# Operands of three products stored as high and low parts by one phase and loaded by the next, and one set of inner weights formed in place

## The chip, the core and the metric

The kernel runs on one core of a Trainium2 chip. The metric is device time in microseconds (us) of one launch; the median of the runs shown is what counts. The core has a matrix engine (PE; its weight loads are listed as PEld), a vector engine (DVE), a scalar engine (ACT), GpSimd (POOL) and SyncE (SP). SP, ACT and POOL can issue transfers between DRAM and the on-chip memory; each engine works through its own instructions in order and waits on semaphores.

## The reference, cut to what matters

```python
def rms_norm(x, w):
    xf = x.astype(jnp.float32)
    y = xf * lax.rsqrt(jnp.mean(xf * xf, axis=-1, keepdims=True) + RMS_EPS)
    return (y * w.astype(jnp.float32)).astype(x.dtype)

def pool_mixer(h, in_w, group_w, group_b, scale, out_w):
    b, s, _ = h.shape
    u, gate = jnp.split(h @ in_w, 2, axis=-1)
    ug = u.reshape(b, s, POOL_GROUPS, POOL_GROUP_DIM)
    pooled = jnp.stack([trailing_mean(ug[:, :, g], w) for g, w in enumerate(POOL_WINDOWS)],
                       axis=2) - ug
    mixed = jnp.einsum('bsgc,gcd->bsgd', pooled, group_w) + group_b
    y = mixed.reshape(b, s, POOL_WIDTH) * scale * jax.nn.silu(gate)
    return y @ out_w
```

There is one layer: h = x + pool_mixer(rms_norm(x, norm_w), ...), and the output is rms_norm(h, final_norm_w). The input has 4096 rows of 1024 float32 values; `in_w` is 1024 x 2048, `out_w` 1024 x 1024, and the trailing windows are 2, 4, 8 and 16 rows long. The mixer's group map is folded into the first half of `in_w`.

## The kernel before, in words

**Precision.** A float32 matmul is made of three: each operand is split into a high part (an ACT copy to float32r) and a low part (a DVE subtraction), and `mm3` adds high x high, high x low and low x high. `split` (L154) does this for one tile of 128 x 1024, with its ACT copy on L152 and its DVE subtraction on L146 (helpers: all ACT copies stand on L152, all DVE subtractions on L146, all additions on L143, all products of two tiles on L149).

**Seven products.** Each matrix product of 2 x 2 blocks is done with seven products instead of eight (the Strassen-Winograd scheme), called P1 to P7. On the data side the sums are S3 (P7), S2 (P6), S1 (P5) and S4 (P3); P1, P2 and P4 take blocks as they are. The code keeps the blocks in `xs[b]` under "11", "12", "21" (which becomes S3), "22" and "2" (S2); "11" becomes S1 and "12" becomes S4, in place.

**Phases.** `steps` (L1171) lists the whole work, one product a step. Phase a (28 steps): four blocks of 1024 rows against one half of the folded input weights. Phase b (28 steps): the same four blocks against the other half. Phase o (56 steps): eight blocks of 512 rows against the output weights. In this text a0 to a3 and b0 to b3 are the blocks of a and b. One product of a or b is 48 matmuls of 128 x 512.

**Phase a to phase b.** Phase a loads the rows of x, normalizes them, forms the sums and splits them. The blocks "11", "12", S3 and "22" of every row block are saved in DRAM (`sd`, as plain float32, L484, on ACT's queue; on POOL's in a0). Phase b loads those four again (`load_saved`, SP's queue) and then forms S2 (L538), S1 (L543) and S4 (L571) and splits them as phase a did.

**Inner products.** In phase b the products P1 and P7 are done by seven smaller products each (`inner_product`, L694; 84 matmuls of 128 x 256 on L676, weights in the tiles `wi`). They run inside the step before: T1 (for P1 of the next block) in the step of P3, T7 (T3 in the change's title, for P7) in the step of P6. Fill units of that step stand between them. Between the inner matmuls ACT copies one part of a bank to others (L701, L707) and DVE adds (L712, L718), so PE waits for ACT and DVE here. Their operands are split by `split_inner` into single `op` tiles, at high priority.

**Inner weights.** `form_wi` makes the seven split inner weights of T1 during a1 and of T7 during a2, in five parts: it loads the raw weights (for T7 from `t3d`), forms four differences (`sums_wi`, two tiles, which it stores to `wt` and loads again), splits each weight (`store_wi`: ACT copy, DVE subtraction, 128 x 512) and stores it to `wid`. In phase b `load_wi` loads all seven into `wi` on POOL's queue (L734) before each use, since T1 and T7 share the tiles.

**Tiles and order.** There are eight `op` tiles (a product holds four, and an inner product's weights one each), 11 `st` and 8 `vt` tiles of 128 x 1024 for everything else; each kind is given out oldest first, and a tile that is still being read by a transfer holds up its next writer. Loads are asked for three steps ahead, splits one step ahead. A scheduler places the instructions on each engine's queue by when it thinks them ready; `high_priority` and `issue_after` bend that order. The end of a product is its eviction, `evict_in` (L921): ACT copies or DVE additions from the banks to `st` or `vt` tiles, which the causal pooling (`pool`, L838) reads and whose product it stores to `yd`. `square_row`, `stats`, `store_rs` and `load_rstd` prepare the row norms of the next block in phase a, with POOL arithmetic and two POOL transfers on the way.

Of the kernel before, what the change touches and what calls it, by code (L numbers as in the profile page):

```python
# [15 lines left out]
P = 128  # L16
# [45 lines left out]
def kernel(  # L62
# [91 lines left out]
    def split(dst, src):  # L154
# [22 lines left out]
        for i in range(P1, P7 + 1)  # L177
# [3 lines left out]
            i: [dram.tile([P, 2, H], F32, name=f"sd{b}_{i}_{h}") for h in range(2)]  # L181
            for i in (P1, P2, P7, P4)
        }
        for b in range(NB)
# [292 lines left out]
    def split_halves(us, saved=None, by_pool=False):  # L477
# [8 lines left out]
        return ts  # L486

    def load_x(b, half, kh):
        us = []
        for h in range(2):  # L490
            u = take()
            k = 4 * kh + 2 * h
            nc.sync.dma_start(out=u, in_=xt[2 * b + 1 - half, :, k : k + 2, :])
            us.append(u)
        return us
# [12 lines left out]
    def load_in(q, b, i):  # L508
        s = xs[b]
        if i == P1:  # L510
            s["11"] = load_saved(b, P1) if q else load_x(b, 0, 0)
        elif i == P2:
            s["12"] = load_saved(b, P2) if q else load_x(b, 0, 1)
        elif i == P7 and swapped(q, b):
            s["21"] = load_x(b, 1, 0)
        elif i == P6:
            if not swapped(q, b):
                s["21"] = load_saved(b, P7) if q else load_x(b, 1, 0)
            s["22"] = load_saved(b, P4) if q else load_x(b, 1, 1)

    def form_in(q, b, i):

        s = xs[b]
        if i in (P1, P2):
            if q == 0:
# [21 lines left out]
    def split_in(q, b, i):  # L547
        s = xs[b]
        key = {P1: "11", P2: "12", P6: "2", P7: "21", P5: "11", P4: "22", P3: "12"}[i]
        if q and i in INNER:  # L550
            inner.update(us=s[key], sums={}, ops={})
            with tc.high_priority():
                split_inner(M_ORDER[:4])
            return None
        later = q == 0 and b == 0 and i in (P1, P2)
        t = split_halves(s[key], None if q or later else sd[b].get(i), b == 0)
        if later:
# [136 lines left out]
    def inner_product(i, sets, fill):  # L694
# [10 lines left out]
        with tc.high_priority():  # L705
            for c in range(2):
                copy(m7[:, c], v22[c])  # L707
        fill.pop(0)()
# [26 lines left out]

    wt = [dram.tile([P, 2, 2, H // 2], F32, name=f"wt{n}") for n in range(4)]
    formed = {}

    def sums_wi(i):
# [6 lines left out]
        with tc.issue_after(latest_split[0]):  # L746
# [3 lines left out]
            sub(t[1][:, 1], b21, t[0][:, 1])  # L750
        for n, u in enumerate(t):
            nc.sync.dma_start(out=wt[n if i == P1 else 2 + n], in_=u)
            give(u)
        store_wi(i, {P1: b11})
        give(us[0])
        formed.update({P2: b21, P3: b22, "held": us[1]})

    def store_wi(i, src):
        behind, after = latest_split[0], evicted[0]
        for m, b in src.items():  # L760
            u = take("p (s a b) -> p s a b", s=2, a=2)
            r = u.bitcast(F32R)
# [4 lines left out]
            nc.sync.dma_start(out=wid[i][M_ORDER.index(m)], in_=u)  # L767
            give(u)

    def load_wt(i, n):  # L770
        u = formed["t", n] = take("p (m a b) -> p m a b", m=2, a=2)
        nc.sync.dma_start(out=u, in_=wt[n if i == P1 else 2 + n])

# [431 lines left out]
    def run(n, between=None, behind=None):  # L1205
# [9 lines left out]
        elif is_inner(n + 1):  # L1215
# [11 lines left out]
            give_ops(t[1])  # L1227
            if steps[n + 1][2] == P7:
                for u in xs[steps[n + 1][1]].pop("21"):
                    give(u)  # L1230
            evict_in(b, 0 if kind == "a" else 1, i, sets)
        else:
# [131 lines left out]
    for h in range(2):  # L1364
# [71 lines left out]
    for n in range(2, len(steps)):  # L1436
# [144 lines left out]
```

## Time and profile before

| what | us |
|---|---|
| median of the 3 runs | 962.76 |
| profiled execution, its own time | 964.31 |
| span from its first to its last instruction | 962.5 |
| PE busy in the span | 914.5 |
| DVE busy | 757.6 |
| ACT busy | 494.9 |
| POOL busy | 82.1 |

The profile is of one execution. It gives, for each engine, what it did and what ended the idle time before an instruction ("DVE op <- ACT op": DVE waited for ACT). A busy PE is not always a fast one: the granted clock (PEclk) stands beside it as a share of full speed. A stage's own rows tell more than the whole span's shares, since phase o at the end has other limits than phases a and b. Block a1 lies at about 107 to 179 us, a2 at 179 to 256, a3 at 256 to 333, then b0 to 422, b1 to 498, b2 to 577, b3 to 665, and phase o to the end; those times are read off the matmul rows.

### The profile page before, as it was taken

Reading aid. Unit: us, or ns where it says so; the run is one execution under the profiler, and the core shown is the slowest. Engines: PE = TensorE matmul, PEld = TensorE weight load, DVE = VectorE, ACT = ScalarE, POOL = GpSimd, SP = SyncE. Lnnn points to the kernel's source line nnn. Section 1 sums busy time; section 2 is a strip of 40 time slices with the busy share of each in tenths; the row PEclk is TensorE's granted clock in tenths of the full one; section 3 lists DMA queues with packets and bytes.
Section 4 is the critical chain, followed back from the end, with each engine's and each line's share of the span. In section 5 each row is a group of like instructions: output and inputs, shape, how many; then the busy total and the mean of one; then the engine's idle time right before and its main releaser. Section 6 shows DMA issues by size and latency. Waiting matters only on the chain. (4 is left out here: it accounts for less than half of the span.)

```text
span 962.5 us, 12330 instructions
## 1 busy us (share of the span) xinstructions
PE 914.5 (95%) x4500; PEld 803.6 (83%) x4500; DVE 757.6 (79%) x890; ACT 494.9 (51%) x857; POOL 82.1 (9%) x186
## 2 busy tenths in 40 slices
PE   9999999998999886989998997899999999999997
PEld 7888888887888775979987986798888888888886
DVE  3898986894995979589498769879988677676675
ACT  6868557446446355446654636566254234234243
POOL 0024001000100010100101101000011011011010
PEclk9999999999999988999998999999999999999999
DMA  9977748997979374724965797663685365365222
GB/s 350 396 285 238 286 175 293 382 326 260 325 265 334 114 241 155 256 85 157 370 229 166 258 354 224 221 193 122 226 297 171 125 227 167 129 223 171 88 88 87
DMA packets 77755, 217.98 MB, mean 226 GB/s; under 512 B 7296, under 2 KB 25088, under 8 KB 77696
## 3 DMA queue, kind: packets, MB, share of 16 engines
q1 hardware_dynamic: 63056, 166.32, 49.0%
q0 software_dynamic: 10464, 37.24, 12.1%
q10 hardware_dynamic: 4176, 13.65, 3.7%
q8 instruction: 35, 0.57, 0.2%
q14 instruction: 24, 0.20, 0.1%
HBM read 146.91 MB, written 70.27 MB: 226 GB/s over the span
## 5 line engine op out<-in xcount | busy, mean ns | idle before, releaser
L593 PE MATMUL bank<-op,w 128*128 128x512 f32 x2304 | 513.0, 383 | 16.2 <-DVE op L146 9.4
L593 PEld LDWEIGHTS bank<-op,w 128*128 128x128 f32 x2304 | 436.7, 191 | 80.7 <-DVE op L146 10.8
L593 PE MATMUL bank<-w,op 128*128 128x512 f32 (+1 forms) x1356 | 290.3, 377 | 0.0
L593 PEld LDWEIGHTS bank<-w,op 128*128 128x128 f32 x1356 | 254.6, 189 | 35.8
L152 ACT ACTIVATE op<-st 128x1024 fp32r<-128x1024 f32 (+1 forms) x148 | 136.1, 928 | 181.7 <-PE bank L593 99.9
L146 DVE TENSOR_TENSOR op<-st,op 128x1024 fp32r<-128x1024 f32 (+1 forms) x148 | 155.7, 1062 | 30.9 <-ACT op L152 23.3
L676 PE MATMUL bank<-op,wi 128*128 128x256 f32 x672 | 90.6, 292 | 23.8 <-ACT bank L152 15.5
L676 PEld LDWEIGHTS bank<-op,wi 128*128 128x128 f32 x672 | 88.3, 205 | 28.6 <-ACT bank L152 16.7
L152 ACT ACTIVATE op<-vt 128x1024 fp32r<-128x1024 f32 (+1 forms) x58 | 55.5, 959 | 88.2 <-PE bank L593 64.6
L152 ACT ACTIVATE vt<-bank 128x512 f32<-128x512 f32 (+1 forms) x94 | 52.7, 584 | 43.7 <-PE bank L593 26.0
L146 DVE TENSOR_TENSOR op<-vt,op 128x1024 fp32r<-128x1024 f32 (+1 forms) x58 | 63.7, 1099 | 10.0 <-ACT op L152 9.3
L1135 DVE TENSOR_TENSOR st<-bank,st 128x512 f32<-128x512 f32 x62 | 42.3, 687 | 28.3 <-PE bank L593 28.1
L146 DVE TENSOR_TENSOR st<-st,st 128x1024 f32<-128x1024 f32 (+2 forms) x41 | 42.4, 1048 | 18.6 <-ACT st L239 13.4
L734 POOL DMA_DIRECT2D wi<-wid x56 | 30.2, 540 | 311.3 <-PE bank L676 277.0
L152 ACT ACTIVATE bank<-bank 128x512 f32<-128x512 f32 (+1 forms) x64 | 33.1, 525 | 19.6 <-PE bank L676 7.6
L873 DVE TENSOR_TENSOR_SCAN vt<-vt,bf 128x512 f32<-128x512 f32 x28 | 34.7, 1270 | 3.6 <-ACT vt L152 3.6
L152 ACT ACTIVATE st<-bank 128x512 f32<-128x512 f32 (+1 forms) x52 | 27.2, 544 | 18.3 <-DVE st L149 5.2
L1135 DVE TENSOR_TENSOR vt<-bank,vt 128x512 f32<-128x512 f32 (+1 forms) x35 | 23.4, 672 | 14.1 <-PE bank L593 13.8
L201 POOL TENSOR_SCALAR oms<-oss 128x2 f32<-128x2 f32 x14 | 9.2, 656 | 292.5 <-ACT st L1024 151.9
L146 DVE TENSOR_TENSOR st<-vt,st 128x512 fp32r<-128x512 f32 (+2 forms) x21 | 17.5, 842 | 17.5 <-ACT st L152 11.3
L143 DVE TENSOR_TENSOR vt<-bank,vt 128x512 f32<-128x512 f32 (+1 forms) x45 | 29.3, 675 | 1.7 <-PE bank L593 1.5
L895 DVE SCALAR_TENSOR_TENSOR vt<-vt,vt 128x1024 f32<-128x1024 f32 x24 | 29.1, 1214 | 0.0
(144 smaller groups left out, 701.1 us busy)
## 6 DMA issues: line engine op xcount, KB each, us to landing
wi<-wid POOLq DMA_DIRECT2D x56, 512.0 KB, 6.0
st<-in_x SPq DMA_DIRECT2D x41, 512.0 KB, 5.4
st<-in_xt SPq DMA_DIRECT2D x27, 512.0 KB, 7.9
st<-sd SPq DMA_DIRECT2D x26, 512.0 KB, 5.6
sd<-st ACTq DMA_DIRECT2D x21, 512.0 KB, 6.2
yd<-st SPq DMA_DIRECT2D x19, 512.0 KB, 4.1
st<-yd SPq DMA_DIRECT2D x18, 512.0 KB, 4.0
out<-st SPq DMA_DIRECT2D x18, 512.0 KB, 3.4
```

The costliest lines, as they stand in the source:

```text
L143: nc.vector.tensor_tensor(out=dst, in0=a, in1=b, op=ALU.add)
L146: return nc.vector.tensor_tensor(out=dst, in0=a, in1=b, op=ALU.subtract)
L152: return nc.scalar.activation(dst, src, func)
L201: nc.gpsimd.tensor_scalar(out=ms, in0=ss, scalar1=1.0 / D, scalar2=EPS, op0=ALU.mult, op1=ALU.add)
L593: latest[0] = nc.tensor.matmul(ps, a, b, start=start and n == 0, stop=stop and n == 2, skip_group_check=True).ins
L676: latest[0] = nc.tensor.matmul(ps, wm[:, sw, kk, cols_of], t[:, sr, kk].rearrange("p (s a) -> p a s", s=2), start=False, stop=kk == 1 and ...
L734: nc.gpsimd.dma_start(out=wi[m], in_=wid[i][m].bitcast(F32R))
L873: nc.vector.tensor_tensor_scan(s[:, j, at:end], v[:, j, at:end], v[:, j, at - win : end - win], sums_of[j] if sums_of else 0.0, ALU.add, A ...
L895: nc.vector.scalar_tensor_tensor(out=s[:, :, at : at + H], in0=s[:, :, at : at + H], scalar=1.0 / win, in1=v[:, :, HIST:], op0=ALU.mult, o ...
L1135: partial["added"] = nc.vector.tensor_tensor(out=dst, in0=src, in1=dst, op=ALU.add).ins
```

## The change

Three things are changed.

1. Phase a stores the split operands of P6 (S2), P5 (S1) and P3 (S4) of every block in DRAM, high and low parts, in new buffers `od` (four transfers of 512 KB for a product, POOL's queue, straight from the `op` tiles). Phase b no longer forms or splits these: `load_ops` loads the four tiles of a product on POOL's queue when phase b would have split them. `form_in` does nothing in phase b, and the tiles of "11", "12", "21" and "22" are given back right after their only use there.
2. The inner weights of T7 are no longer formed in a2. The load of their raw parts stands after a3's P3, and the four sums and seven splits after b0's P1 and P2, with the splits written straight into `wi`. They are stored to `wid` from there on POOL's queue, for b1 to b3. `sums_wi` and `store_wi` hold both cases in the diff. The sums are no longer stored to `wt` and loaded again, and b0 has no `load_wi` for T7.
3. In a step with an inner product, the eviction of the step's own product is put behind the two ACT copies of L707 in ACT's queue.

```diff
+    od = [
+        {
+            i: [
+                [dram.tile([P, 2, H], F32, name=f"od{b}_{i}_{h}_{s}") for s in range(2)]
+                for h in range(2)
+            ]
+            for i in (P6, P5, P3)
+        }
+        for b in range(NB)
+    ]
...
+    def save_ops(b, i, ts):
+        for h, t in enumerate(ts):
+            for s, u in enumerate(t):
+                nc.gpsimd.dma_start(out=od[b][i][h][s], in_=u.bitcast(F32))
+
+    def load_ops(b, i):
+        ts = []
+        for h in range(2):
+            t = next_op(2)
+            for s, u in enumerate(t):
+                nc.gpsimd.dma_start(out=u, in_=od[b][i][h][s].bitcast(F32R))
+            ts.append(t)
+        return ts
...
+        elif q:
+            if i == P7:
+                s["21"] = load_saved(b, P7)
+            elif i == P4:
+                s["22"] = load_saved(b, P4)
         elif i == P6:
             if not swapped(q, b):
-                s["21"] = load_saved(b, P7) if q else load_x(b, 1, 0)
-            s["22"] = load_saved(b, P4) if q else load_x(b, 1, 1)
+                s["21"] = load_x(b, 1, 0)
+            s["22"] = load_x(b, 1, 1)
 
     def form_in(q, b, i):
         s = xs[b]
+        if q:
+            return
...
+        if q and i in (P6, P5, P3):
+            return load_ops(b, i)
+        if q:
+            t = split_halves(s[key])
+            for u in s.pop(key):
+                give(u)
+            return t
         later = q == 0 and b == 0 and i in (P1, P2)
-        t = split_halves(s[key], None if q or later else sd[b].get(i), b == 0)
+        t = split_halves(s[key], None if later else sd[b].get(i), b == 0)
+        if i in (P6, P5, P3):
+            save_ops(b, i, t)
...
             for c in range(2):
-                copy(m7[:, c], v22[c])
+                inner["copied"] = copy(m7[:, c], v22[c]).ins
...
+        if i == P1:
+            for n, u in enumerate(t):
+                nc.sync.dma_start(out=wt[n], in_=u)
+                give(u)
+        else:
+            formed["t", 0], formed["t", 1] = t
...
+            if i == P1:
+                u = take("p (s a b) -> p s a b", s=2, a=2)
+                r = u.bitcast(F32R)
+            else:
+                r = wi[n]
+                u = r.bitcast(F32)
             with tc.issue_after(behind):
                 with tc.issue_after(after):
                     copy(r[:, 0], b)
                 sub(r[:, 1], b, u[:, 0])
...
+            else:
+                nc.gpsimd.dma_start(out=wid[i][n], in_=u)
...
-            if steps[n + 1][2] == P7:
-                for u in xs[steps[n + 1][1]].pop("21"):
-                    give(u)
-            evict_in(b, 0 if kind == "a" else 1, i, sets)
+            for u in xs[steps[n + 1][1]].pop("21" if steps[n + 1][2] == P7 else "11"):
+                give(u)
+            with tc.issue_after(inner["copied"]):
+                evict_in(b, 0 if kind == "a" else 1, i, sets)
...
+    save_ops(0, P6, split_up[2])
...
-        if kind == "a" and b in (1, 2):
+        if kind == "a" and b == 1:
             k = ORDER_LATER.index(i) - 1
             if 0 <= k < 5:
-                form_wi(P1 if b == 1 else P7, k)
+                form_wi(P1, k)
+        elif kind == "a" and b == NB - 1 and i == P3:
+            form_wi(P7, 0)
+        elif kind == "b" and b == 0 and i in (P1, P2):
+            for k in (1, 2) if i == P1 else (3, 4):
+                form_wi(P7, k)
...
-        if kind == "b" and i == P2:
+        if kind == "b" and i == P2 and b > 0:
             load_wi(P7)
```

More of the change, by code (lines that the diff above doesn't have):

```diff
@@ L734, in load_wi @@
             nc.gpsimd.dma_start(out=wi[m], in_=wid[i][m].bitcast(F32R))
-    wt = [dram.tile([P, 2, 2, H // 2], F32, name=f"wt{n}") for n in range(4)]
+    wt = [dram.tile([P, 2, 2, H // 2], F32, name=f"wt{n}") for n in range(2)]
     formed = {}
@@ L750, in sums_wi @@
             sub(t[1][:, 1], b21, t[0][:, 1])
-        for n, u in enumerate(t):
-            nc.sync.dma_start(out=wt[n if i == P1 else 2 + n], in_=u)
-            give(u)
+        formed.update({P2: b21, P3: b22, "held": us[1]})
+        if i == P1:
[4 more added lines that the diff above has]
+            formed["t", 0], formed["t", 1] = t
         store_wi(i, {P1: b11})
         give(us[0])
-        formed.update({P2: b21, P3: b22, "held": us[1]})
     def store_wi(i, src):
@@ L760, in store_wi @@
         for m, b in src.items():
-            u = take("p (s a b) -> p s a b", s=2, a=2)
-            r = u.bitcast(F32R)
+            n = M_ORDER.index(m)
+            if i == P1:
[4 more added lines that the diff above has]
+                u = r.bitcast(F32)
             with tc.issue_after(behind):
@@ L766, in store_wi @@
                 sub(r[:, 1], b, u[:, 0])
-            nc.sync.dma_start(out=wid[i][M_ORDER.index(m)], in_=u)
-            give(u)
+            if i == P1:
+                nc.sync.dma_start(out=wid[i][n], in_=u)
+                give(u)
+            else:
+                nc.gpsimd.dma_start(out=wid[i][n], in_=u)
     def load_wt(i, n):
-        u = formed["t", n] = take("p (m a b) -> p m a b", m=2, a=2)
-        nc.sync.dma_start(out=u, in_=wt[n if i == P1 else 2 + n])
+        if i == P1:
+            u = formed["t", n] = take("p (m a b) -> p m a b", m=2, a=2)
+            nc.sync.dma_start(out=u, in_=wt[n])
     def load_t3(h):
@@ L1227, in run @@
             give_ops(t[1])
-            if steps[n + 1][2] == P7:
-                for u in xs[steps[n + 1][1]].pop("21"):
-                    give(u)
-            evict_in(b, 0 if kind == "a" else 1, i, sets)
+            for u in xs[steps[n + 1][1]].pop("21" if steps[n + 1][2] == P7 else "11"):
+                give(u)
+            with tc.issue_after(inner["copied"]):
+                evict_in(b, 0 if kind == "a" else 1, i, sets)
         else:
```

## The prediction

> **What bounds the kernel now.** First the page: who is busy.
>
> ```profile
> PE 914.5 (95%) x4500; PEld 803.6 (83%) x4500; DVE 757.6 (79%) x890; ACT 494.9 (51%) x857; POOL 82.1 (9%) x186
> ```
>
> PE is the bound; only its idle time (962.5 - 914.5 = 48 us) and its slow clock can be won. Next the table of stages, one row a block, to see where:
>
> ```profile
> 33.00:107.00 74.00, 72.15 (x337) 62.46 (x336) 68.29 (x82) 55.12 (x84) 19.86 (x27) 1.00 0.79 285
> 107.00:179.00 72.00, 72.00 (x335) 62.91 (x334) 58.32 (x63) 44.21 (x74) 4.70 (x14) 1.00 0.75 271
> 179.00:256.00 77.00, 72.73 (x328) 62.54 (x327) 59.51 (x66) 38.85 (x69) 5.38 (x13) 0.98 0.89 312
> 256.00:333.00 77.00, 74.37 (x344) 64.24 (x343) 65.10 (x70) 34.84 (x56) 4.36 (x8) 1.00 0.74 263
> 333.00:422.00 89.00, 74.23 (x405) 66.54 (x405) 67.96 (x90) 45.83 (x78) 7.55 (x14) 0.92 0.53 177
> 422.00:498.00 76.00, 73.48 (x413) 66.40 (x412) 59.78 (x74) 42.30 (x85) 7.56 (x14) 0.98 0.74 256
> 498.00:577.00 79.00, 73.86 (x408) 66.58 (x407) 61.88 (x73) 41.84 (x89) 7.54 (x14) 0.96 0.70 245
> 577.00:665.00 88.00, 79.20 (x429) 70.73 (x428) 76.26 (x84) 55.06 (x107) 3.77 (x7) 0.96 0.60 193
> ```
>
> Columns: stretch, length, busy time of PE, PEld, DVE, ACT, POOL, granted clock, share of the transfer engines, GB/s. PE's idle time is length less busy: a1 0, a2 4.3, a3 2.6, but b0 14.8, b1 2.5, b2 5.1, b3 8.8. The clock falls where PE waited: (1 - clock) x length is 1.5 us in a2, 7.1 in b0, 1.5 in b1, 3.2 in b2, 3.5 in b3. So phase b loses 31.2 + 15.3 = 46.5 us, 21.9 of them in b0. PE's waits name the releasers:
>
> ```profile
> PE bank L676 <- ACT bank L152: 15.5, 4, 7.3
> PE bank L593 <- DVE op L146: 9.4, 3, 7.5
> PE bank L676 <- DVE bank L143: 8.2, 3, 3.6
> PE bank L593 <- ACT st L152: 4.5, 2, 3.2
> ```
>
> Rows one and three (23.7 us) are inner products waiting for their copies and additions; row two is mostly P6 of b0 waiting for a low part. No wait of PE here names a transfer. The two longest, in PE's timeline:
>
> ```profile
> 341.62 2.93 PE L676 MATMUL bank<-op,wi 128*128 128x256 f32 x12 [7.29 <-ACT bank L152]
> ...
> 373.88 8.22 PE L593 MATMUL bank<-op,w 128*128 128x512 f32 x26 [7.48 <-DVE op L146]
> ```
>
> The first is explained by ACT's timeline: an eviction waited for a store that was to free its tile, and the bank copies that PE needed stood behind it.
>
> ```profile
> 340.69 0.60 ACT L152 ACTIVATE vt<-bank 128x512 f32<-128x512 f32 x1 [2.81 <-DMA yd<-vt]
> 341.19 0.65 ACT L152 ACTIVATE bank<-bank 128x256 f32<-128x256 f32 x2
> ```
>
> **The change part by part.** All sums stand against the profiled execution, 964.31 us (span 962.5), 1.55 above the median of 962.76; the saving is then taken off the median.
>
> *Forming and splitting in phase b goes.* For each block six sums and six low parts on DVE, six high parts on ACT:
>
> ```profile
> L146 DVE TENSOR_TENSOR op<-st,op 128x1024 fp32r<-128x1024 f32 x35 | 42.2, 1216 | 8.6 <-ACT st L152 5.0 <-ACT vt L152 2.5 <-ACT op L152 1.1
> L146 DVE TENSOR_TENSOR op<-st,op 128x512 fp32r<-128x512 f32 x42 | 27.8, 681 | 4.5 <-ACT op L152 4.4
> ```
> ```profile
> L152 ACT ACTIVATE op<-st 128x1024 fp32r<-128x1024 f32 x105 | 110.2, 1054 | 145.4 <-PE bank L593 78.3 <-DVE st L149 25.2 <-PE bank L676 24.4
> ```
>
> DVE: 12 x 1.216 = 14.6 us a block, 58 in all; ACT: 6 x 1.054 = 6.3, 25 in all. Neither is PE's bound, so this pays only where PE waits for them. Blocks "11", "12" and S2's tiles are also given back earlier, so evictions and loads find free tiles sooner.
>
> *The eviction behind the m7 copies.* It takes the wait of 341.62 off its present cause. What is late next there is DVE: the inner operands' sums and splits, 0.68 us each, among the pooling of a3. The eviction itself has the rest of the inner product to run in (P6's last fill unit ends just before it), so I cost its delay at nothing.
>
> *b1 to b3.* They lose 2.5 + 1.5, 5.1 + 3.2 and 8.8 + 3.5 = 24.6 us, all at inner products. DVE falls from about 60 busy of 76 to about 45. But the pooling of the block's other half still falls at T1, with scans of 1.27 us that an addition for PE has to wait out:
>
> ```profile
> L873 DVE TENSOR_TENSOR_SCAN vt<-vt,bf 128x512 f32<-128x512 f32 x28 | 34.7, 1270 | 3.6 <-ACT vt L152 3.6
> ```
>
> So some waits stay: I take 17 of 24.6 (bounds 5 and 24.6).
>
> *T7's inner weights.* In a2 the wait of 3.2 us goes with its cause, and 1.5 of clock: 4.7 us.
>
> ```profile
> DVE st L146 <- DMA vt<-t3d: 4.0, 1, 4.0
> ...
> ACT st L152 <- DMA wt<-st: 3.5, 1, 3.5
> ...
> PE bank L593 <- ACT st L152: 3.2, 1, 3.2
> ```
>
> In b0 the work comes back: 4 sums and 7 low parts, 11 x 0.68 = 7.5 us on DVE, before T7. This stretch, from T1's start to T7's, is the tightest of the kernel:
>
> ```profile
> 333.00:382.00 49.00, 34.23 (x181) 30.44 (x181) 43.30 (x56) 26.55 (x45) 3.78 (x7) 0.86 0.54 173
> ```
>
> DVE is busy 43.3 of 49 us. Out of it go P6's sums and low parts (4 x 1.216) and the S4 and S1 sums done early (3 x 1.216), 8.5 us; 7.5 come in: 42.3. Unbroken, DVE would have T7 ready at 333 + 42.3 = 375.3, against 382 now; some of its work there (phase b's own P3 and P4 weights) can fall behind T7, while breaks push it back. PE without waits would need T7 by about 364: T1 takes 14 us as T7 does (rows below), P2's 48 matmuls 48 x 72.0 / 335 = 10.3, P6's first five units 6.5, from 333 on. So b0 keeps one long wait, at T7 instead of P6. I take 382 - 375.3 = 6.7 and a third of b0's 7.1 of clock: 9 us (bounds 0, when DVE's breaks stay, and 21.9, when all fits).
>
> *Stores in phase a.* 48 transfers of 0.524 MB, 25.2 MB, 6.3 a block. The trace has no store from an `op` tile; the nearest rows are POOL's loads, 0.54 us of POOL each, and the transfer engines when they are full:
>
> ```profile
> L734 POOL DMA_DIRECT2D wi<-wid x56 | 30.2, 540 | 311.3 <-PE bank L676 277.0 <-PE bank L593 34.1 <-issue 0.2
> L457 POOL DMA_DIRECT2D vt<-rd x6 | 3.4, 570 | 31.7 <-DMA rd<-rs 31.7
> ```
> ```profile
> DMA packets 2920, 8.75 MB, mean 381 GB/s; under 512 B 274, under 2 KB 274, under 8 KB 2919
> ## 3 DMA queue, kind: packets, MB, share of 16 engines
> q1 hardware_dynamic: 1911, 5.07, 63.0%
> q0 software_dynamic: 1008, 3.67, 42.7%
> ...
> wi<-wid POOLq DMA_DIRECT2D x7, 512.0 KB, 8.5
> ```
>
> (The second fence is the transfer view of 459 to 482 us, T7 of b1: full, at 381 GB/s.) So a block's stores take 6.3 / 0.381 = 16.5 us of all engines, 66 in phase a. The stages leave free 0.21 x 74 + 0.25 x 72 + 0.11 x 77 + 0.26 x 77 = 62 us, and a2 loses the traffic of forming T7 (7 + 2 + 2 + 2 transfers, 6.8 MB, 18 us): 80 against 66. It fits, without much to spare. An `op` tile is written again only after its product (10.3 us) and after its store has read it; the store, issued at the split before that product, has at least those 10.3 us, against 8.5 to land in the full row. Behind the stores on POOL stand the norms' arithmetic and their two small transfers, a step ahead of their use by the code's order; the load already waits 31.7 / 6 = 5.3 us each time, and nobody waits for it. I take 2 us (bounds 0 and 33, half of the stores).
>
> *Loads in phase b.* The same 25.2 MB. P3's follow P5's tiles and have a product to land in; P6's have all of P2. P5's are the short ones: their `op` tiles come free inside T7, and P5 starts when T7 ends. T7 has 84 matmuls of L676 and three fill units:
>
> ```profile
> 381.94 2.95 PE L676 MATMUL bank<-op,wi 128*128 128x256 f32 x24
> 384.73 1.46 PE L593 MATMUL bank<-op,w 128*128 128x512 f32 x6
> ```
>
> 84 x 2.95 / 24 + 3 x 1.3 = 14 us. In them `load_wi` for the next T1 asks for 3.7 MB on the same queue. In that full stretch 2.1 MB more take 2.1 / 0.381 = 5.5 us. If it all shows, with half as much again in clock, b0 to b2 lose 3 x 8 = 24; if served first, 0. I take 1 + 3 + 3 = 7. Next-block loads on SP (x, saved blocks, output weights) lie behind the same engines; they are asked for three steps ahead.
>
> *Sum.* 4.7 + 9 + 17 - 2 - 7 = 21.7: 964.3 becomes 942.6, and on the median **941.1 us**.
>
> The Trainium skill, "DMA: Bandwidth & Descriptors", section "Issuing engines are not separate DMA queues", says that transfers from SP, ACT and POOL run on the same 16 engines and interleave, so POOL's queue adds no bandwidth; the shares above, 63.0% and 42.7% together over the whole, agree. The same page's limit of about 358 GB/s for HBM would make an estimated 70 us of the stores; the 381 measured decides.
> The Trainium skill, "TensorE: Matmul & The Clock Gate", section "Part 1: The HAM clock gate", has the clock halve after an idle window of about 3.4 us. The trace differs: b1's only wait on PE was 2.5 us and its clock is 0.98. By the page b1's 1.5 us would not be there to win, and the estimated sum would be about 1 us less.
>
> **The rivals.**
> 1. *Phase a runs out of transfer time* (slower). For it: a2 stands at 0.89 now, and 66 of the 80 us of room are spoken for. Against: no wait of PE in phase a names a transfer. If half of the 66 us shows, 941.1 - 2 + 33 = 972. It beats the gain from 23.7 us on, 36% of the stores, and makes it 2% slower (982) from 65%.
> 2. *P5's operands come late after T7*: a new wait of PE on a transfer in b0, b1 and b2. For: the full stretch at T7. Against: freer tiles let SP's loads go earlier. 941.1 - 7 + 24 = 958.
> 3. *All is hidden*: b0 to b3 lose nothing and the transfers cost nothing, 962.8 - 46.5 - 4.7 = 912. For: DVE's load in b1 to b3. Against: b0's DVE.
> 4. *The change moves b0's wait, not less of it*: the 7.5 us land in the same stretch, b0 gains 0: 950. It lies within my range for the forecast.
>
> **How the numbers follow.** Forecast, with the fourth, 0.48, its own range 927 to 955; all hidden 0.22; P5 late 0.15; phase a full 0.15. The 2% bounds are 943.5 and 982.0 (about what a measurement of this kernel can tell from no change). Faster: 0.22 and 0.30 of the forecast's 0.48, 0.52. Slower: 0.10, two thirds of phase a's case, where more than 65% shows or P5's case comes with it (972 + 17 = 989). Same: the rest, 0.38. The range runs from all hidden, 912, to phase a nearly half exposed, 970.
>
> **What would show it.** Right: phase b's rows of DVE near 45 to 60, PE's wait at 341 short and no longer on an eviction, P6 of b0 without a wait on a low part, a2 without its 3.2. A wait of PE at T7 of b0 on a DVE low part of `wi`. Wrong: waits of PE with a transfer from `od` as releaser (rival 2), or in a1 and a3 ACT copies to `op` that wait for `od` stores (rival 1).

## The result, and the profile after

| | before | after |
|---|---|---|
| median, us (11 executions each, same chip) | 962.52 | 971.33 |
| ratio to before, 95% interval | | 1.0098 [1.0078, 1.0119] |
| profiled execution, us (span) | 964.31 (962.5) | 971.33 (969.5) |

The change makes the kernel 1% slower. The forecast was 941.1, with a range from 912 to 970: wrong in sign, and outside the range. One of the executions of the kernel before was a slow one of 1185.74 us; the ratio leaves it out, and without it the median of before would be 0.4 us lower.

First the page of the kernel after, who is busy, and POOL's transfer queue (packets, MB, share of the 16 engines).

```profile
PE 919.7 (95%) x4500; PEld 805.2 (83%) x4500; DVE 705.4 (73%) x842; ACT 471.7 (49%) x833; POOL 128.5 (13%) x282
...
q0 software_dynamic: 24288, 87.58, 25.1%
```

DVE fell by 52 us (757.6 before) of the 58 that were forecast, and PE got nothing for it. The queue carries the 50 MB that the stores and loads were to add (10464 packets and 37.24 MB before). Next the table of stages of the kernel after, with the columns of the prediction's table. The stretches are those of before, so a late row holds a little of the block ahead of it.

```profile
33.00:107.00 74.00, 70.52 (x320) 60.49 (x319) 61.75 (x72) 52.25 (x79) 19.63 (x38) 0.98 0.92 353
107.00:179.00 72.00, 69.93 (x317) 60.68 (x316) 57.85 (x64) 41.46 (x72) 12.42 (x26) 0.98 0.86 313
179.00:256.00 77.00, 72.29 (x332) 62.09 (x331) 56.87 (x59) 38.89 (x65) 12.32 (x26) 1.00 0.99 383
256.00:333.00 77.00, 73.77 (x341) 64.03 (x340) 58.99 (x64) 33.59 (x50) 10.15 (x19) 1.00 0.76 280
333.00:422.00 89.00, 76.80 (x407) 67.60 (x406) 63.29 (x89) 41.67 (x77) 14.57 (x28) 0.92 0.83 290
422.00:498.00 76.00, 70.36 (x394) 62.69 (x394) 48.57 (x66) 36.03 (x76) 13.95 (x26) 0.98 0.84 293
498.00:577.00 79.00, 75.05 (x411) 67.30 (x410) 45.40 (x57) 38.67 (x88) 13.95 (x26) 0.96 0.93 325
577.00:665.00 88.00, 81.64 (x444) 73.20 (x443) 64.95 (x77) 46.88 (x93) 10.21 (x19) 0.96 0.90 310
```

Two things stand out. In a0 and a1 PE is busy 1.6 and 2.1 us less than before, and a2's transfer engines are full (0.99). In b1 and b2 DVE is at 48.6 and 45.4, as forecast, and still the clock is no better and b1's PE stands idle longer (5.6 us against 2.5).

Where the time went is read off the start of each product in PE's timeline, after minus before:

| up to the start of | us later | what lies in that stretch |
|---|---|---|
| P4 of a0 | +3.6 | a wait in P5 of a0 |
| P6 of a1 | +7.5 | a wait in P7 of a1 |
| P2 of a2 | +11.2 | two waits in P1 of a2 |
| P4 of a2 | +6.7 | the wait on T7's forming is gone: -4.5 |
| P6 of a3 | +3.3 | two waits of before in a3 are gone: -3.4 |
| P3 of a3 | +7.1 | two new waits: +3.8 |
| P2 of b0 | +8.3 | T1 of b0: +1.2 |
| P5 of b0 | +4.6 | P6 of b0, with T7 in it: -3.7 |
| P4 of b0 | +6.7 | P5 of b0 waits for its loads: +2.1 |
| P6 of b1 | +10.3 | T1 of b1 and the slow clock behind it: +3.6 |
| P2 of b3 | +11.8 | T1 of b2 and of b3 |
| P5 of b3 | +6.9 | T7 of b3: -4.9 |

From there to the end it stays at +6.9, the difference of the spans. So two forecasts failed: phase a lost some 15 us to something, and b1 to b3 gained nothing (+6.7 to +6.9) where 17 us were forecast. PE's waits in the kernel after (total us, times, longest):

```profile
PE bank L716 <- DVE bank L143: 14.5, 5, 5.0
PE bank L633 <- DVE op L146: 9.0, 6, 2.2
PE bank L716 <- ACT bank L152: 8.2, 5, 4.3
PE bank L633 <- DMA op<-od: 4.2, 1, 4.2
PE bank L633 <- ACT st L152: 2.1, 1, 2.1
```

The waits on ACT's copies fell from 15.5 to 8.2 us, but those on DVE's bank additions rose from 8.2 to 14.5. DVE has less to do and is later where PE needs it. Its own waits on transfers, in the kernel after, say part of why. Before, that list held waits on `yd` and on `in_xt` of 1.7 and 1.6 us, and none on `rd` or `sd<-vt`:

```profile
DVE st L143 <- DMA st<-sd: 10.7, 2, 7.0
...
DVE vt L146 <- DMA yd<-vt: 7.2, 1, 7.2
...
DVE st L146 <- DMA yd<-st: 6.8, 1, 6.8
DVE st L149 <- DMA vt<-rd: 5.4, 2, 3.4
...
DVE st L149 <- DMA st<-in_xt: 4.1, 1, 4.1
...
DVE vt L146 <- DMA sd<-vt: 1.5, 1, 1.5
```

The first row, the longest, lies in T7 of b1 and at the end of T7 of b2, where PE had no wait. The two on `yd` belong to phase b and the last three to phase a. (In a3, ahead of its two new waits, DVE also waits 7.9, 4.4 and 4.5 us for loads of weights; before, 4.8, 1.4 and 3.7 us at the same place.) In phase a, POOL's and DVE's timelines of the kernel after, around the wait in P5 of a0:

```profile
55.31 0.54 POOL L501 DMA_DIRECT2D od<-op  x1 [2.39 <-ACT op L152]
58.12 0.53 POOL L501 DMA_DIRECT2D od<-op  x1 [2.27 <-DVE op L146]
58.65 0.53 POOL L494 DMA_DIRECT2D sd<-st  x1
60.47 0.54 POOL L501 DMA_DIRECT2D od<-op  x1 [1.29 <-ACT op L152]
62.30 0.53 POOL L501 DMA_DIRECT2D od<-op  x1 [1.29 <-DVE op L146]
...
65.63 0.55 POOL L1520 DMA_DIRECT2D sd<-vt  x1
```
```profile
77.54 1.23 DVE L146 TENSOR_TENSOR vt<-vt,early 128x1024 f32<-128x1024 f32 x1 [1.53 <-DMA sd<-vt]
```

The same store of a saved block in the kernel before:

```profile
59.38 0.53 POOL L1467 DMA_DIRECT2D sd<-vt  x1
```

In the kernel after this store (`sd<-vt`) stands behind four new stores in POOL's queue. Before each of them POOL waits for a split (2.39, 2.27, 1.29 and 1.29 us), so it is issued 6.2 us later than before. It lands 11.9 us after its issue, where it took 8.3 before. DVE, which is to write that tile, waits, and the split that PE needs stands behind. The small transfer of the norms does worse. The rows of the transfer view and of POOL's waits, in the kernel after (the view is of 33 to 107 us):

```profile
rd<-rs POOLq DMA_DIRECT2D x2, 2.0 KB, 10.6
```
```profile
POOL vt L467 <- DMA rd<-rs: 47.3, 6, 11.6
```

2 KB take 10.6 us to land, against 3.9 in the same stretch before; POOL's wait for them rose from 31.7 to 47.3 us in all, and now somebody waits for it (DVE on `vt<-rd`, 5.4).

In phase b, DVE's and PE's timelines of the kernel after, in T1 of b1:

```profile
436.65 0.76 DVE L143 TENSOR_TENSOR bank<-bank,st 128x256 f32<-128x256 f32 x2
437.32 1.22 DVE L146 TENSOR_TENSOR op<-st,op 128x1024 fp32r<-128x1024 f32 x1
445.77 0.69 DVE L146 TENSOR_TENSOR vt<-st 128x512 f32<-128x512 f32 x1 [7.23 <-DMA yd<-vt]
446.38 0.68 DVE L143 TENSOR_TENSOR vt<-st,st 128x512 f32<-128x512 f32 x1
446.98 0.42 DVE L143 TENSOR_TENSOR bank<-bank,st 128x256 f32<-128x256 f32 x1
```
```profile
447.46 1.82 PE L716 MATMUL bank<-op,wi 128*128 128x256 f32 x11 [3.44 <-DVE bank L143]
```

The subtraction at 445.77 is the first sum of the *next* inner product, T7. T7 runs in the step of P6, which starts 15 us later. But DVE is idle, so it is placed early, ahead of the bank addition at 446.98 that PE waits for. Its output tile is still being read by the store of the block's other half (`yd<-vt`, issued at 436.77, which lands 8.9 us later in a stretch of 371 GB/s), and DVE works in order: 7.23 us of waiting for nothing urgent. In b2 the same happens at 524.36, 6.8 us. Behind these two stand PE's waits of 3.4 and 2.1 us. PE's longest wait, 5.0 us in T1 of b3, has no wait of DVE on a transfer before it: there DVE is busy from 594.1 to 599.5 with pooling and the first sums of T7, all ahead of the addition.

### The profile page after: what moved, and what is told of

It reads as the page before. It is cut to its first block, busy times and chain, and to the rows that moved or that the text cites. A ratio compares the mean times of both kernels' runs of the same rounds, so it can differ in the third digit from the quotient of the medians.

```text
span 969.5 us, 12416 instructions
## 1 busy us (share of the span) xinstructions
PE 919.7 (95%) x4500; PEld 805.2 (83%) x4500; DVE 705.4 (73%) x842; ACT 471.7 (49%) x833; POOL 128.5 (13%) x282
## 4 chain that ended last, share of the span: by engine, by line
PE 54%; DVE 16%; DMA 16%; issue 6%; ACT 5%; POOL 1%; ACTq 0%; DVEq 0%; SPq 0%; POOLq 0%
PE bank L633 48%; PE bank L716 5%; DVE op L146 3%; DVE st L149 2%; DVE vt L143 2%; DMA rd<-rs 2%; DMA yd<-vt 2%; DVE st L146 1%; DMA st<-sd 1%; DMA wid<-st 1%; ACT op L152 1%; DMA sd<-vt 1%; DMA yd<-st 1%; DMA vt<-rd 1%; DVE vt L146 1%
## 5 line engine op out<-in xcount | busy, mean ns | idle before, releaser
L633 PE MATMUL bank<-op,w 128*128 128x512 f32 x2304 | 517.2, 385 | 17.8 <-DVE op L146 9.0
L152 ACT ACTIVATE op<-st 128x1024 fp32r<-128x1024 f32 (+1 forms) x125 | 111.2, 899 | 180.7 <-PE bank L633 129.5
L146 DVE TENSOR_TENSOR op<-st,op 128x1024 fp32r<-128x1024 f32 (+1 forms) x125 | 127.2, 1028 | 41.9 <-ACT op L152 38.9
L716 PE MATMUL bank<-op,wi 128*128 128x256 f32 x672 | 89.8, 289 | 23.8 <-DVE bank L143 14.5
L716 PEld LDWEIGHTS bank<-op,wi 128*128 128x128 f32 x672 | 86.0, 201 | 30.3 <-DVE bank L143 17.2
L1187 DVE TENSOR_TENSOR st<-bank,st 128x512 f32<-128x512 f32 x60 | 41.0, 686 | 30.3 <-PE bank L633 30.1
L774 POOL DMA_DIRECT2D wi<-wid x49 | 26.4, 539 | 154.8 <-PE bank L716 123.8
L501 POOL DMA_DIRECT2D od<-op x48 | 26.1, 544 | 142.7 <-ACT op L152 96.7
L508 POOL DMA_DIRECT2D op<-od x48 | 25.8, 540 | 114.7 <-PE bank L716 50.4
L146 DVE TENSOR_TENSOR st<-st,st 128x1024 f32<-128x1024 f32 (+2 forms) x32 | 32.1, 1020 | 8.0 <-DMA st<-wvd 4.5
L1187 DVE TENSOR_TENSOR vt<-bank,vt 128x512 f32<-128x512 f32 (+1 forms) x37 | 24.8, 673 | 12.0 <-PE bank L633 11.7
```

The lines of the kernel that those rows point to most:

```text
L146: return nc.vector.tensor_tensor(out=dst, in0=a, in1=b, op=ALU.subtract)
L152: return nc.scalar.activation(dst, src, func)
L501: nc.gpsimd.dma_start(out=od[b][i][h][s], in_=u.bitcast(F32))
L508: nc.gpsimd.dma_start(out=u, in_=od[b][i][h][s].bitcast(F32R))
L633: latest[0] = nc.tensor.matmul(ps, a, b, start=start and n == 0, stop=stop and n == 2, skip_group_check=True).ins
L716: latest[0] = nc.tensor.matmul(ps, wm[:, sw, kk, cols_of], t[:, sr, kk].rearrange("p (s a) -> p a s", s=2), start=False, stop=kk == 1 and ...
```

## The experiments

Two theories stood first. **The stores**: phase a's 48 stores cost what b's gain can't pay back (the prediction's first rival). **Phase b itself**: T7's forming in b0, or the changed order of the evictions, spoils the gain. Where an expectation uses a letter, A is the theory of the stores' bytes; what stands against it is told there. Each ratio below is to the kernel before on the same chip; its median lies between 962.4 and 963.9 on all of them, and differences to the kernel after are differences of medians.

**1. The stores alone.** The kernel before, with phase a's stores and nothing that reads them.

```diff
+        if q == 0 and i in (P6, P5, P3):
+            save_ops(b, i, t)
...
+    save_ops(0, P6, split_up[2])
```

> The kernel before, with phase a's 48 stores of split operands added on POOL's queue and nothing that reads them; phase b as before. Theory A (the stores cost phase a its time, by their bytes and by the queue they share): 969 to 975, with PE's new waits in a0's P5, a1's P7 and a2's P1, some 8 to 11 us by a2's P2. Rival O (the time comes from the new order of instructions that the scheduler made, not from transfers): 960 to 965. Rival B (all of the loss is in phase b): 962.

992.03 us, 1.0279 [1.0239, 1.0318], far above the range of theory A. The cost is 29 us, with T7's forming still in a2; P2 of b0 starts 30.3 us late and nothing more is lost behind it. a2's row and PE's waits, in this kernel:

```profile
179.00:256.00 77.00, 64.63 (x267) 54.24 (x266) 54.15 (x57) 37.36 (x59) 8.34 (x16) 0.89 0.97 356
```
```profile
PE bank L610 <- DVE op L146: 24.4, 10, 7.7
```

In a2 PE is busy 64.6 of 77 us, and over the whole kernel ten waits on low parts take 24.4 us (9.4 in three before). With T7's forming in place the prediction's balance was 62 us of free transfer time against 66: by it some 4 us would be missing, not 29. Nor is it one full block alone: by the starts of the products a2 loses 11.6 us and a3 12.0, though the balance had 0.26 of a3's 77 us (20 us) free for stores of 16.5. A sum of free transfer time doesn't tell the price here.

**2. Half the bytes.** The kernel after, where each store and load of `od` moves half of its tile; the other half of the operands of P6, P5 and P3 isn't the reference's.

```diff
-                nc.gpsimd.dma_start(out=od[b][i][h][s], in_=u.bitcast(F32))
+                nc.gpsimd.dma_start(out=od[b][i][h][s][:, 0:1], in_=u[:, 0:1].bitcast(F32))
...
-                nc.gpsimd.dma_start(out=u, in_=od[b][i][h][s].bitcast(F32R))
+                nc.gpsimd.dma_start(out=u[:, 0:1], in_=od[b][i][h][s][:, 0:1].bitcast(F32R))
```

> The changed kernel, but each store and each load of a split operand moves only the first half of its tile (256 KB instead of 512 KB, as many transfers); the other half of each operand in phase b is left from earlier work, so the three products' sums leave half of their terms wrong. Theory A: phase a's loss halves or better and the waits of DVE on stores at T1 of b1 and b2 get shorter: 950 to 961. Rival O (order): nothing moves, 967 to 973.

956.02 us, 0.9921 [0.9893, 0.995]: 15.3 us under the kernel after, with the same instructions. At P2 of b0 it stands 4.1 us ahead of before, where the kernel after stands 8.3 behind. As many transfers, issued by the same instructions but with half the bytes, cost little.

**3. Without the part on T7.** The kernel after, with T7's weights formed in a2 as before.

```diff
-        if kind == "a" and b == 1:
+        if kind == "a" and b in (1, 2):
             k = ORDER_LATER.index(i) - 1
             if 0 <= k < 5:
-                form_wi(P1, k)
+                form_wi(P1 if b == 1 else P7, k)
```

> The changed kernel with T7's inner weights formed in a2 as before. Theory A: a2 gets its old wait of 3 to 5 us back, with the forming's 6.8 MB on top of the stores, and b0 loses 7.5 us of DVE work: 970 to 982. Rival T (forming T7's weights in b0 is what eats the gain of the loads): 950 to 962.

975.51 us, 1.0121 [1.0092, 1.015]. At P2 of b0 it stands 26.1 us behind before, so in phase a the part on T7 is worth 17.8 us to the change (26.1 - 8.3): far more than the 4.7 forecast, with the stores and the forming's transfers in a2 together. In phase b this kernel gains 17.0 us (26.1 to 9.1), where the change gains 1.4. So the rest of the change brings phase b nearly the net sum that was forecast (26 - 7 = 19), though in other shares: 8.2 in b0 and 8.8 in b1 to b3. With the part on T7, 15.6 of it is gone: 4.5 in P6 and T7 of b0 (-8.2 here, -3.7 after), 2 at P5 of b0, which here has no wait on `od`, and 9 in b1 to b3. How those 9 come about is not shown. DVE has no wait on a `yd` store in this kernel's list, yet PE waits 14.0 us for DVE's bank additions here too (14.5 after). In b1 to b3 PE's waits add up to 11.7 us (15.8 after), and the stretches at half clock to 6.8 us (17.1 after).

**4. The order of the evictions alone**, on the kernel before.

```diff
-                copy(m7[:, c], v22[c])
+                inner["copied"] = copy(m7[:, c], v22[c]).ins
...
-            evict_in(b, 0 if kind == "a" else 1, i, sets)
+            with tc.issue_after(inner["copied"]):
+                evict_in(b, 0 if kind == "a" else 1, i, sets)
```

> The kernel before with the third part alone: the eviction behind the m7 copies. The prediction's step: the wait of 7.3 us in T1 of b0 shrinks to 2 to 5, the smaller ones by less: 955 to 960. Rival: DVE's splits of T1 and P6 of b0 take the time back: 961 to 964.

962.63 us, 0.9992 [0.997, 1.0014]. The wait of 7.3 us in T1 of b0 falls to 3.6, and then 1.2 more wait at P6 (8.6 for 7.5) and 1.0 at the operands' splits. It is worth nothing alone, as the rival said.

**5. The stores on SP's queue.** The kernel after, with one word changed.

```diff
-                nc.gpsimd.dma_start(out=od[b][i][h][s], in_=u.bitcast(F32))
+                nc.sync.dma_start(out=od[b][i][h][s], in_=u.bitcast(F32))
```

> The changed kernel with phase a's 48 stores issued from SP's queue instead of POOL's; the bytes are the same. If the bytes set the price (theory A1): 966 to 975, as the changed kernel. If POOL's in-order queue sets it, with its waits for splits ahead of other stores and of the norms' transfers (theory A2): phase a's waits in a0's P5 and a1's P7 go, 957 to 964; SP's own loads may then be held up by the same waits, which would speak for the queue as well, with 980 or more.

962.95 us, 1.0005 [0.9984, 1.0026]: 8.4 us under the kernel after with the same bytes. P6 of a1 stands at +2.1 instead of +7.5. POOL's wait for the small transfer, in this kernel:

```profile
POOL vt L467 <- DMA rd<-rs: 34.5, 5, 8.7
```

It is nearly back at its 31.7. a2's engines are as full as in the kernel after, so what is saved is not bandwidth. In a0 the store `sd<-vt` is issued at 59.45, 6.2 us sooner than in the kernel after, since POOL has no splits to wait for ahead of it. It takes longer to land (14.6 us for 11.9), though POOL's queue holds none of the new stores, and is still there 3.5 us sooner. So in a0 the move saves POOL's waits ahead of the issue, and the slow landing stays. One wait of PE of 3.3 us is left in a2. Ahead of it DVE waits 5.8 us for a load on SP's queue (`in_xt`); whether the full engines or the stores that now share that queue make it late was not separated.

```profile
179.00:256.00 77.00, 73.66 (x334) 63.52 (x333) 57.56 (x60) 39.32 (x65) 5.67 (x15) 0.98 1.00 387
```

**6. Stores in a3 only.** The kernel after without the stores of a0 to a2; phase b takes a3's S2, S1 and S4 for every block.

```diff
-        if i in (P6, P5, P3):
+        if i in (P6, P5, P3) and b == NB - 1:
...
-                nc.gpsimd.dma_start(out=u, in_=od[b][i][h][s].bitcast(F32R))
+                nc.gpsimd.dma_start(out=u, in_=od[NB - 1][i][h][s].bitcast(F32R))
...
-    save_ops(0, P6, split_up[2])
```

> The changed kernel, but only a3's split operands are stored, and phase b loads those for every block (so three blocks of three products use another block's sums); phase b's loads, order and work are as in the changed kernel. Theory A (36 of the 48 stores cost phase a its time): some 11 us of waits in a0 to a2 go and a2 keeps its gain of 4.5: 951 to 958. Rival O (order, not transfers): 967 to 973.

959.34 us, 0.9959 [0.9937, 0.998], 1.3 us above theory A's range. The stores of a0 to a2 cost 12.0 us. But without them the change still gains only 3 us: at P2 of b0 it stands 3.3 ahead, at the end 1.4. The loss in phase b is there without them.

**7. T7's sums behind T1's additions.** The kernel after with one edge of order on DVE: the first four operands of T7 are formed and split after the last addition of the inner product before.

```diff
-                add(v22[c], v12[c], m7[:, c])
+                inner["added"] = add(v22[c], v12[c], m7[:, c]).ins
...
-            with tc.high_priority():
+            behind = inner.get("added")
+            with tc.issue_after(behind) if behind else nullcontext(), tc.high_priority():
```

> The changed kernel with one order edge: the sums and splits of an inner product's operands stand behind the last additions of the inner product before on DVE's queue. In the changed kernel DVE waits 7 us in T1 of b1 and b2 for a store to free the tile of T7's first sum, and PE's additions stand behind it. If that order is where the loads' gain went (theory B1): the waits of 2.2, 3.4, 1.9, 2.1 and 5.0 us in T1 of b1 to b3 fall to a third, with their slow clock: 955 to 964. If PE's wait only moves to T7, whose operands come later (rival): 968 to 976.

965.4 us, 1.0038 [1.0022, 1.0054]: 5.9 us under the kernel after, between the two ranges. Phase b now gains 11.0 us (from +10.8 at P2 of b0 to -0.15). Of PE's five waits the two that stood behind a waiting DVE are gone (3.4 and 2.1 us); 2.2 and 1.9 stay, and 5.0 falls to 3.3. In T1 of b1, DVE's timeline of this kernel:

```profile
445.37 0.43 DVE L143 TENSOR_TENSOR bank<-bank,st 128x256 f32<-128x256 f32 x1 [3.88 <-PE bank L717]
446.04 0.43 DVE L143 TENSOR_TENSOR bank<-bank,st 128x256 f32<-128x256 f32 x1 [0.24 <-PE bank L717]
449.00 0.69 DVE L146 TENSOR_TENSOR vt<-st 128x512 f32<-128x512 f32 x1 [2.53 <-DMA yd<-vt]
```

The additions stand ahead of the sum and wait for PE, not PE for them; PE has no wait at what the sum still waits for its tile.

**8. Plain sums.** The kernel after with S2, S1 and S4 stored as plain float32, half the bytes, on ACT's queue (a0's S2 on POOL's), loaded on SP's and split in phase b.

```diff
-            for i in (P1, P2, P7, P4)
+            for i in (P1, P2, P7, P4, P6, P5, P3)
...
-        if q and i in (P6, P5, P3):
-            return load_ops(b, i)
...
-        if i in (P6, P5, P3):
-            save_ops(b, i, t)
```

> The changed kernel, but S2, S1 and S4 are stored as plain float32 (half the bytes) on ACT's queue, as the other blocks are, loaded on SP's queue, and split in phase b; so only the six sums of a block are saved there, not its splits. Theory A: phase a's price halves, phase b keeps 6 of 12 DVE instructions a block: 952 to 962. Rival (the splits were what phase b needed rid of): 965 to 975.

970.68 us, 1.0081 [1.005, 1.0112]. It lies in the range of the rival, not of theory A. The splits are back on DVE and ACT in phase b, which loses 3.3 us (+4.0 at P2 of b0, +7.3 at the end), and a3 has one new wait of 6.1 us on a low part, in P6, whose cause I did not separate. With the splits back in phase b, half the bytes don't make the change pay.

**9. Both cures**: the stores on SP's queue (5) and the edge (7).

> Both cures in one: the stores on SP's queue and the inner sums behind the last additions. If the two losses are separate, phase a's by POOL's queue (8 us) and phase b's by DVE's order (6 us), they add up: 971.3 - 8.4 - 5.9 = 957, range 954 to 960. If they overlap (the one's wait hides the other): 960 to 965.

953.7 us, 0.9894 [0.9876, 0.9913], 10.2 us under the kernel before and 17.6 under the kernel after. The two gains add up (8.4 and 5.9 by themselves), with 3.3 us more. P2 of b0 stands 1.8 ahead of before, the end 13.1 (the profiled execution, 950.94 us, is the fastest of the six). Two rows of its table of stages, a2 and b3:

```profile
179.00:256.00 77.00, 73.48 (x327) 63.59 (x326) 56.78 (x59) 39.26 (x64) 5.10 (x14) 0.96 1.00 380
...
577.00:665.00 88.00, 85.37 (x462) 76.27 (x461) 69.43 (x77) 49.92 (x92) 9.69 (x18) 1.00 0.81 281
```

PE's waits on DVE's bank additions, in this kernel:

```profile
PE bank L717 <- DVE bank L143: 6.9, 4, 2.6
```

14.5 us in the kernel after. DVE is no less busy here (705.3 us for 705.4): the gain comes from order and waits, not from less work.

**10. And T7's weights stored on SP's queue.** As 9, with `nc.sync` in place of `nc.gpsimd` for the stores of `wid` in b0.

> The same with the seven stores of T7's weights in b0 on SP's queue too. PE's only long wait on a transfer from the new buffers is P5 of b0 (4.2 us and its clock), whose loads stand behind those stores on POOL's queue. By the queue theory that wait goes: 2 to 6 us less than the run without it, 950 to 955. If P5's loads are late by the full engines alone: no change, 954 to 960.

952.25 us, 0.9884 [0.9865, 0.9902]. The wait of P5 of b0 on `od`, 5.4 us in 9, falls to 0.7 and 2.0; against 9 the time can't be told apart. It is the lowest of the study.

**11. The same stores, an eighth of the bytes.** The kernel after; the stores of a0 to a2 stand in POOL's queue where they stood, but move 64 KB each. Phase b takes a3's tiles for every block, as in 6.

```diff
-                nc.gpsimd.dma_start(out=od[b][i][h][s], in_=u.bitcast(F32))
+                full = b == NB - 1
+                part = (slice(0, 2 if full else 1), slice(0, H if full else 128))
+                nc.gpsimd.dma_start(
+                    out=od[b][i][h][s][:, part[0], part[1]],
+                    in_=u[:, part[0], part[1]].bitcast(F32),
+                )
```

> The changed kernel with all 48 stores on POOL, in the same places and with the same waits, but those of a0 to a2 move one eighth of their bytes (64 KB), and phase b loads a3's operands for every block (so the sums of three blocks are another block's). If POOL's waits for the splits set the price, whatever the bytes: 967 to 973, as the changed kernel. If it is the bytes in POOL's queue: 955 to 962, as with the stores of a0 to a2 left out.

960.71 us, 0.9959 [0.9938, 0.9979], the same as 6. POOL issues as many transfers and waits for the same splits, and the losses of a0 and a1 are gone (4.0 and 3.9 us in the kernel after, together 0.5 here). In a0 the store `sd<-vt` is issued at 64.38, nearly as late as in the kernel after, but lands 5.5 us later instead of 11.9. With experiment 5 that makes two causes in a0, of which taking away either is enough: POOL's waits ahead of the issue, and bytes that slow the landing. It doesn't hold for a2: P1 of a2 loses 4.5 us here too, with an eighth of the bytes (3.6 in the kernel after), so there the stores' bytes are not shown to be the cause.

**12. The edge of 7 on the kernel before.**

> A control: the kernel before with the order edge alone (inner sums behind the last additions of the inner product before). In the kernel before DVE has no wait on a store in T1 of b1 to b3, so if the edge cures a wait that the change made, nothing moves: 960 to 965. If it cures what was there all along: 955 to 959.

961.66 us, 0.9994 [0.9978, 1.0011]. The edge has nothing to mend there: it cures a wait that the change made.

## Why the prediction was wrong, point by point

- *Stores in phase a: "I take 2 us (bounds 0 and 33)"*. **Failed.** By the table above they cost some 15 us in phase a: 4.0 in a0 (which stood 0.4 ahead), 3.9 in a1, 3.6 in a2, 3.8 in a3 (experiment 6 has 12.0 for those of a0 to a2, all told). Two steps were wrong. "It fits", the balance of 80 us of room against 66 for the whole of phase a, does not tell what the stores cost: a0 and a1 lose 4.0 and 3.9 us at shares of 0.92 and 0.86. And of the queue the text said that behind the stores stand two small transfers "a step ahead of their use ... nobody waits for it"; the same queue also holds a0's `sd` stores, which POOL now issues 6.2 us later, behind its waits for splits, and when the 2 KB land after 10.6 us instead of 3.9 the step ahead is used up. Experiments 5 and 11 show this: the same bytes on another queue, or fewer bytes on the same one, take most of the losses in a0 and a1 away (7.9 us in the kernel after, 2.1 and 0.5 there). For the losses in a2 and a3 the cause stays open; DVE waits there for loads on SP's queue.
- *b1 to b3: "I take 17 of 24.6 (bounds 5 and 24.6)"*. **Failed**, and below its bound: they gained nothing. DVE's load fell as forecast. The step that failed is the inference from a busy share to a wait: an idle DVE took T7's first sum early, ahead of the additions, and stood at a tile that a store was reading. Experiment 7 shows this for two of PE's five waits and gains 5.9 us, 12 shows that before had none of it, and in 9, with the stores on SP's queue as well, b1 to b3 gain 12.4 us.
- *T7's inner weights in b0: "9 us (bounds 0 ... and 21.9)"*. The direction held: P6's wait on a low part is gone and T7's wait on `wi` is 0.9 us. From T1's start to P5 the gain is 2.5 us (-3.7 in P6 with T7, +1.2 in T1); experiment 3, without the forming there, gains 4.5 more in P6 with T7. The mechanism was right, the size not. With the wait at P5 that follows, 0.4 us are left of it at P4 (+7.1 to +6.7).
- *The eviction, cost nothing, T1's wait taken off its present cause*. The releaser is another, as forecast, but three waits of 6.4 us in all stay in T1 of b0. Late next is DVE, yet not with the splits that the text named: ACT clears banks for the inner product, and waits for DVE's additions that empty them. ACT's timeline of the kernel after:

```profile
340.91 0.39 ACT L152 ACTIVATE bank<-zero 128x256 f32<-128x256 f32 x1 [5.01 <-DVE st L143]
342.64 0.39 ACT L152 ACTIVATE bank<-zero 128x256 f32<-128x256 f32 x1 [1.35 <-DVE st L143]
...
346.24 0.39 ACT L152 ACTIVATE bank<-zero 128x256 f32<-128x256 f32 x1 [0.89 <-DVE st L143]
```

Alone the part is worth nothing (experiment 4).
- *T7's forming leaves a2: 4.7 us*. 4.5 in the kernel after. With the stores in place the part on T7 is worth much more: 17.8 us over phase a (experiment 3). The two parts of the change can't be priced apart.
- *Loads in phase b: "1 + 3 + 3"*. The wait on `od` at P5 was forecast, and comes in b0 alone: 4.2 us, behind the stores of `wid`. POOL's timeline of the kernel after:

```profile
386.51 0.53 POOL L819 DMA_DIRECT2D wid<-wi  x1
387.43 1.78 POOL L819 DMA_DIRECT2D wid<-wi  x3 [0.39 <-DVE wi L146]
389.21 0.55 POOL L508 DMA_DIRECT2D op<-od  x1
390.71 0.55 POOL L508 DMA_DIRECT2D op<-od  x1 [0.96 <-PE bank L633]
```

- The rivals: the first, "phase a runs out of transfer time", came nearest, with nearly half of its price (15 of 33 us), but not by the path of its sign: ACT's copies to `op` waited for an `od` store once, 0.6 us, and moving the stores to SP's queue saves 8.4 us with the same bytes. It was said to beat the gain from 23.7 us on; 15 sufficed, since the gain it had to beat did not come. The second came true in b0 alone (4.2 us), the fourth nearly so: b0 gains 0.4 us in all. None of the four had DVE's new order in b1 and b2.
- The clock. The Trainium skill, "TensorE: Matmul & The Clock Gate", section "Part 1: The HAM clock gate", was weighed at about 3.4 us of idleness. The trace differs again: the wait of 2.01 us in a0 is followed by 3.4 us at half clock. PE's timeline and the table of stages of the kernel after:

```profile
80.02 4.33 PE L633 MATMUL bank<-op,w 128*128 128x512 f32 x11 [2.01 <-DVE op L146]
```
```profile
80.40:83.80 3.40, 3.40 (x10) 2.68 (x9) 2.97 (x3) 3.40 (x8) 2.95 (x6) 0.50 0.66 130
```

So a wait that a queue makes costs more than its own length: 4.0 us in a0 for a wait of 2. What decides can be read from the traces: the half-clock stretches of a trace all start a whole number of slots of 3.413 us apart, and PE's idle time within one slot decides on the next. In the kernel after, the slots 77.0 to 80.4 and 513.9 to 517.3 have 2.0 and 1.9 us of idleness and a slow slot behind them. The waits of 2.2 us at 192 and 435 are divided by a slot's border (1.9 with another wait, then 1.3; 0.4, then 1.8) and have none. Over the 14 traces, from 40 to 940 us, every full-clock slot with over 2.02 us of idleness is followed by a slow one, none with under 1.7 us is, and between the two both occur.
- The Trainium skill, "DMA: Bandwidth & Descriptors", section "Issuing engines are not separate DMA queues", says that another issuing engine saves only sequencer time. For bandwidth this case agrees (a2 full either way). For time it doesn't: SP in place of POOL was worth 8.4 us, 971.33 to 962.95, in a0 since other transfers of POOL's queue no longer stand behind its waits for the splits.

What stays open: the cause of the losses in a2 and a3 (3.6 and 3.8 us, and a2's 3.3 us with the stores on SP), how the part on T7 takes 9 us from b1 to b3, the wait of experiment 8 in a3, and how much of a3's own gain (3.4 us) comes from T7's leaving a2.

## What to carry to other kernels

Free transfer time, summed over stages, did not tell what added transfers cost here: look at what stands behind them on the *same* queue, both behind their bytes and behind the issuing engine's waits for their sources. A small transfer or a store that frees a tile is late there, and then its reader is. An engine that gets less to do doesn't give its time to the waiting one by itself; a scheduler fills it with early work, and if that work's tile is still being stored, an in-order engine stops in front of what is urgent. So when a change frees an engine, ask which instruction now moves ahead of the one that matters, and pin that order.

## What the runs showed that was not expected

- A 2 KB transfer lands after 10.6 us on a queue with big stores ahead of it, 3.9 before (a0's stretch), and 7.4 with those stores on another queue (experiment 5): about half of the delay doesn't come from sharing the queue.
- Waits of PE of 1.9 to 2.1 us (at 78, 136, 514 and 525 us of the kernel after) were followed by 3.4 us at half clock; the prediction's shortest was 2.5. Others of 2.2 us (at 192 and 435) were not: what counts is the idleness within one slot of 3.413 us.
- A DVE with 16 us less work in a stretch (b2: 45.4 for 61.9) kept PE waiting longer on its additions, 14.5 us for 8.2 in all.
